# Other transfer estimates in an issue planner, and y loads on strands of their own

## The chip, the cores and the metric

One program runs on one core of one Trainium2 chip. The metric is the time of one execution in microseconds (us) on the device. Engines are named as the profile names them: PE (matmul), PEld (the weight loads that go with it), DVE (vector), ACT (scalar), POOL (GpSimd) and SP, whose queue issues all DMAs of this kernel.

## The reference

Two layers of a backbone. Each layer normalises 256 context rows and 1024 latent rows of width 1024, projects them into the inputs of four mixers, joins the four results to y, and projects y back:

```python
for l in range(DEPTH):                       # 2 layers
    need_ctx = l < DEPTH - 1
    ...                                      # mod, sh, sc, gt from c and c_ctx
    hx = _rms(x, norm_w[l]) * (1.0 + sc[:, None, :]) + sh[:, None, :]
    hc = _rms(ctx, norm_w[l]) * (1.0 + sc_c) + sh_c
    ux = _split(hx @ w_in[l], [M_COLS, A_COLS, G_COLS, D_COLS])
    uc = _split(hc @ w_in[l], [M_COLS, A_COLS, G_COLS, D_COLS])
    outs = [_mlstm_mixer(...), _diff_mixer(...), _gla_mixer(...), _gdn_mixer(...)]
    yx = jnp.concatenate([o[1] for o in outs], axis=-1)
    x = x + gt[:, None, :] * (yx @ w_out[l])
    if need_ctx:
        yc = jnp.concatenate([o[0] for o in outs], axis=-1)
        ctx = ctx + gt_c * (yc @ w_out[l])
return x
```

The mixers are an mLSTM, a differential attention, a gated linear attention (GLA) and a gated delta net (GDN); each gives 256 of the 1024 columns of y.

## The kernel before

The 1280 rows are ten tiles of 128 (layer 1 needs the eight latent tiles alone). Everything between stages (the projections, the mixers' inputs, y as `yd`, half-finished sums as `xp`) goes through DRAM.

The order of the instructions is not written by hand. While the program is built, each piece of the work is a strand (a thread) with a rank, and the class `Issue` records every operation through its `__call__` (the line L406 on which nearly all instructions of the profile stand). For each it works out, with numbers of its own, how long the operation takes on its engine (`dur`) and when its result can be read (`fin`); `choose` lets the strand go on whose next operation could start first, ranks breaking near ties. What comes out is one fixed list of instructions per engine, and for SP one fixed list of DMAs. These numbers are used only to order; the chip's own waits are semaphores. A strand asks for another's result with `need` and announces its own with `set`. `evac`, `sub` and `mulv` also use the planner's clock to choose between two engines, so the engine of a copy or a product can change with the numbers.

For a DMA the planner takes 0.475 us to issue (`dur`), then a start 0.65 us later or when the transfer ahead of it is through, bytes / 360e3 us of transfer and 1.0 us to land. For an ACT activation it takes a fixed part and an element count; loading the table of another function costs nothing in it.

The output projection has two halves. `out_first` multiplies the columns of attention and GDN (blocks 2, 3, 6, 7 of y) with `w_out`, adds the residual and stores `xp`; it runs beside GLA and the mLSTM. `outproj` does blocks 0, 1, 4, 5 (mLSTM and GLA), adds `xp`, and, in layer 0, normalises the sum for the next layer. Each half loads a tile of y (`out_load`, 128 rows by 512 columns, 256 KB, tile `y`, two buffers), turns it with four transposes on PE (`tr<-k_ident,y`), splits it into `yT` on ACT and DVE (`out_turn`), and multiplies (24 matmuls `o<-w,yT` or `o<-wo,yT`). In both, one strand `turns` does load and turn:

```python
for i in range(n):
    if "m" in parts:
        q_.need((l, "mlstm", i))
    if i > 1:
        q_.need((l, "o", i - 2, 1))
    todo[i] = out_load(L, L.yt[i], ks, op)
    ...
    out_turn(todo[i], ks, op, pps)
```

So the load of tile i stands behind the last matmul of tile i-2, and its turn right behind the load. The mLSTM, which runs at the same time, loads for each tile `pd` (512 KB), `kq` (512 KB), `mv`, `wb` and `oz`, and stores its part of y (`y<-hy`); its matmuls are `pp`, `m`. Other names in the rows: `KT` are the keys of the attention (`sc` its scores), `wm` the modulation weights (`mod`), `raw`, `rtmp`, `gsp` and `al` tiles of the gates' and GDN's front on which ACT runs Ln and Exp, `st` the residual tile of `out_first`, `x` that of `outproj`.

Of the kernel before, what the change touches and what calls it, by code (L numbers as in the profile page):

```python
# [16 lines left out]
AF = mybir.ActivationFunctionType  # L17
# [123 lines left out]
class Issue:  # L141
# [8 lines left out]

    def __init__(self):
        self.cols, self.psum = {}, set()
        self.shape, self.port = None, {"V": collections.deque(maxlen=12), "G": collections.deque(maxlen=12)}
        self.window, self.cool = collections.deque(), False
        self.now = dict.fromkeys("PVSGD", 0.0)
        self.link = 0.0
        self.past, self.slot, self.free = {}, {}, {}
        self.depth, self.gone = {}, {}
        self.done = set()
        self.strands, self.me, self.fault = [], None, None  # L160
        self.main = threading.Semaphore(0)
        self.log = None
# [46 lines left out]
    def note(self, name, box, wrote, end):  # L209
        a, b, c, d = box  # L210
        old = self.past.setdefault(name, [])
        old[:] = [u for u in old if not (u[4] == wrote and u[5] <= end and a <= u[0] and u[1] <= b and c <= u[2] and u[3] <= d)]
        old.append((*box, wrote, end))


    def run(self, *strands):
# [86 lines left out]
                self.give()  # L303
                self.me.wait = None

    def set(self, name):
        self.done.add(name)


    def __call__(self, e, op, fn, a, k):  # L310
# [49 lines left out]
                dur += n * 0.006  # L360
        elif e == "S":
            dur = (0.05 if op == "copy" else 0.09) + n / 1200 + (0.09 if "accum_out" in k or "bias" in k else 0)
        elif e == "G":
            r = 2.2 if op == "tensor_tensor" else 0.85 if op == "memset" else 0.93
            if ALU.pow in a:
                r = 165
            dur = 0.12 + n * r / 1000
        else:
            dur = 0.475
# [19 lines left out]
        end = start + dur  # L389
        if port:  # L390
            self.port[e].append((start, end))
        if e == "D":
            self.link = max(self.link, end + 0.65) + math.prod(outs[0][2].shape) * 4 / 360e3
            fin = self.link + 1.0
        else:
            fin = end + self.LAG[e]
        self.now[e] = end
# [32 lines left out]
def _build(tc, nc, A, out, root, dbg):  # L430
# [2225 lines left out]
    def out_first(L, wp, end):  # L2656
# [27 lines left out]
        def ev(*k):  # L2684
            return (l, "of", *k)

        def turns():
            mark(f"{l}out.first")
            for i in n:
                if i > 1:  # L2690
                    q_.need(ev("p", i - 2, 1))
                bs[i] = out_load(L, L.yt[i], ks, O.p)
                out_turn(bs[i], ks, O.p, O.ps)
                bs[i].ps = {}
                q_.set(ev("yT", i))

        def evacs():
            mark(f"{l}out.first")
# [7 lines left out]
            for i in n:  # L2706
# [10 lines left out]
                    q_.set(ev("e", i, nh))  # L2717
                dma(xp[l][128 * t:128 * t + 128, :], xs[i])
                q_.set((l, "first", t))
        q_.spawn(RANK["first turn"], turns)  # L2720
        q_.spawn(RANK["first turn"], evacs)
        for i in n:
# [11 lines left out]
    def outproj(L):  # L2734
# [5 lines left out]
        with ExitStack() as st:  # L2740
# [17 lines left out]
            def turns():  # L2758
                mark(f"{l}out.turn")
                for i in range(n):  # L2760
                    if "m" in parts:
                        q_.need((l, "mlstm", i))
                    if i > 1:
                        q_.need((l, "o", i - 2, 1))
                    todo[i] = out_load(L, L.yt[i], ks, op)
                    todo[i].i, todo[i].ps = i, {}
                    out_turn(todo[i], ks, op, pps)
                    q_.set((l, "yT", i))
                q_.set((l, "turns"))

            def place(t):
                g = next(g for g, (t0, n_) in enumerate(GRP) if t0 <= t < t0 + n_)
# [82 lines left out]
            def finishes():  # L2855
# [10 lines left out]
                for i, t in enumerate(L.yt):  # L2866
# [13 lines left out]
                    else:  # L2880
                        dma(x1[t], b.x)
                    q_.set((l, "fins", i))
            q_.spawn(RANK["out turn"], turns)
            q_.spawn(RANK["out turn"], finishes)
            if end:
# [55 lines left out]
```

## Time and profile before

| | |
|---|---|
| median of 3 runs | 2452.58 us (2437.7 to 2453.14) |
| profiled execution | 2444.86 us, its span 2443.0 us |
| PE busy | 2141.1 us (88% of the span) |
| DVE, ACT, POOL busy | 1513.1, 987.4, 850.4 us |
| DMA | 335.37 MB, 137 GB/s in the mean |
| chain that ended last | PE 55%, DMA 13%, DVE 11%, issue 8%, ACT 6%, SP queue 5% |
| mean granted clock of TensorE | 0.937 |

The span runs from the first instruction to the last. Busy shares are means over stages with different limits: layer 0 ends at about 1365 us, and in each layer the stage with the mLSTM and the output projection comes last.

### The profile page before, as it was taken

What the parts mean: (1) busy time and instruction counts of PE and PEld (TensorE: products, weight loads), DVE (VectorE), ACT (ScalarE), POOL (GpSimd) and SP (SyncE); (2) the same over time, 40 slices, a digit from 0 to 9 for tenths busy, and PEclk for the clock granted to TensorE, in tenths of its full rate; (3) what the DMA queues carried; (4) which work ended last, traced back from release to release, by engine and by line L of the source; (5) the groups of instructions that cost most, each with busy time, mean ns of one, the idle gap of its engine ahead of it and who ended that gap; (6) DMA issues with size and microseconds to landing.
All of it is one profiled execution on the core that took longest, in us unless ns stands there. A gap on an engine that the chain in (4) does not pass through costs nothing.

```text
span 2443.0 us, 57689 instructions
## 1 busy us (share of the span) xinstructions
PE 2141.1 (88%) x23367; PEld 1762.3 (72%) x23367; DVE 1513.1 (62%) x2676; ACT 987.4 (40%) x2169; POOL 850.4 (35%) x1075
## 2 busy tenths in 40 slices
PE   5899999999898998886868798889999989977888
PEld 1656778888776687865756677888888667866776
DVE  3586679555386854546556396686642778555665
ACT  2346412333376853222424255412322677533240
POOL 1343523554122225241522163623442122254340
PEclk8899999999999999988989899999999999976989
DMA  7347643455513134157953135432444331353694
GB/s 260 116 133 228 198 140 109 138 152 157 143 46 91 51 84 147 51 143 213 279 178 133 43 124 173 158 113 93 148 149 126 91 100 38 75 152 85 186 277 172
DMA packets 348051, 335.37 MB, mean 137 GB/s; under 512 B 93146, under 2 KB 292282, under 8 KB 347274
## 3 DMA queue, kind: packets, MB, share of 16 engines
q1 hardware_dynamic: 347786, 331.69, 45.6%
q8 instruction: 185, 3.03, 0.5%
q14 instruction: 80, 0.66, 0.1%
HBM read 226.78 MB, written 107.43 MB: 137 GB/s over the span
## 4 chain that ended last, share of the span: by engine, by line
PE 55%; DMA 13%; DVE 11%; issue 8%; ACT 6%; SPq 5%; POOL 2%; ACTq 0%; POOLq 0%; DVEq 0%
PE mm L406 26%; PE po L406 5%; SPq L406 5%; PE tr L406 4%; PE o L406 4%; PE sc L406 3%; PE p L406 3%; PE pd L406 3%; DVE st L406 2%; DMA wm<-in_w_mod 2%; PE puw L406 2%; ACT p L406 2%; PE m L406 2%; DVE cacc L406 1%; DMA KT<-akh 1%
## 5 line engine op out<-in xcount | busy, mean ns | idle before, releaser
L406 PE MATMUL mm<-w,hT 128*128 128x256 f32 x4512 | 645.6, 294 | 20.7 <-DVE st L406 10.0
L406 PEld LDWEIGHTS mm<-w,hT 128*128 128x128 f32 x4512 | 580.9, 195 | 52.9 <-issue 20.4
L406 PE MATMUL mm<-hT,w 128*128 128x512 f32 (+1 forms) x1680 | 388.9, 377 | 19.0 <-DVE w L406 4.9
L406 PEld LDWEIGHTS mm<-hT,w 128*128 128x128 f32 x1680 | 283.1, 195 | 90.0 <-issue 19.6
L406 DVE TENSOR_REDUCE st<-sc 128x1 f32<-128x1024 f32 (+1 forms) x200 | 200.2, 1027 | 69.8 <-PE sc L406 68.3
L406 ACT ACTIVATE p<-sc,st 128x256 f32<-128x256 f32 (+1 forms) x272 | 211.3, 786 | 68.8 <-DVE st L406 54.8
L406 POOL TENSOR_TENSOR w<-wr,w 128x512 fp32r<-128x512 f32 x62 | 87.4, 1411 | 235.5 <-ACT w L406 199.4
L406 POOL TENSOR_TENSOR hss<-hss,mhalf 128x2 f32<-128x2 f32 (+2 forms) x72 | 105.7, 1467 | 181.7 <-DVE hss L406 175.8
L406 PE MATMUL o<-wo,yT 128*128 128x512 f32 x540 | 155.2, 425 | 8.6 <-DVE x L406 7.1
L406 PE MATMUL sc<-KT,qt 96*128 96x512 f32 (+1 forms) x400 | 124.9, 402 | 30.3 <-DMA KT<-akh 13.3
L406 POOL TENSOR_TENSOR ss<-ss,mhalf 128x1 f32<-128x1 f32 (+1 forms) x39 | 68.2, 1749 | 193.4 <-DVE ss L406 185.4
L406 PEld LDWEIGHTS o<-wo,yT 128*128 128x128 f32 x540 | 105.7, 202 | 34.7 <-issue 5.6
L406 ACT COPY st<-mm 128x512 f32<-128x512 f32 (+1 forms) x83 | 45.8, 552 | 202.0 <-PE mm L406 140.9
L406 ACT COPY wt<-tr 128x512 f32<-128x512 f32 (+1 forms) x200 | 102.2, 511 | 60.4 <-PE tr L406 59.8
L406 PE MATMUL o<-w,yT 128*128 128x512 f32 x324 | 107.3, 462 | 21.8 <-DVE st L406 12.3
L406 PE MATMUL tr<-k_ident,p 128*128 128x128 f32 x656 | 114.7, 280 | 7.5 <-ACT wt L406 7.2
L406 POOL TENSOR_TENSOR st<-st 128x1 f32<-128x1 f32 (+1 forms) x136 | 26.6, 195 | 266.5 <-ACT p L406 196.9
L406 ACT CAST w<-wr 128x512 fp32r<-128x512 f32 x128 | 76.8, 620 | 103.7 <-PE mm L406 52.6
L406 PEld LDWEIGHTS sc<-KT,qt 96*128 96x128 f32 x400 | 63.8, 197 | 60.4 <-ACT p L406 32.0
L406 PE MATMUL po<-wt,av 128*64 128x128 f32 x1312 | 103.0, 282 | 2.0 <-DVE aacc L406 2.0
L406 DVE SCALAR_TENSOR_TENSOR p<-p,st,p 128x1280 f32<-128x1280 f32 (+1 forms) x72 | 103.0, 1431 | 2.6 <-POOL st L406 2.5
L406 DVE TENSOR_TENSOR w<-wr,w 128x512 fp32r<-128x512 f32 x66 | 59.1, 895 | 68.6 <-ACT w L406 64.9
(315 smaller groups left out, 4125.8 us busy)
## 6 DMA issues: line engine op xcount, KB each, us to landing
wr<-in_w_in SPq DMA_DIRECT2D x64, 512.0 KB
wm<-in_w_mod SPq DMA_DIRECT2D x64, 256.0 KB
y<-y SPq DMA_DIRECT2D x36, 256.0 KB
xp<-st SPq DMA_DIRECT2D x18, 512.0 KB
pd<-rs_NG SPq DMA_DIRECT2D x18, 512.0 KB
kq<-kq SPq DMA_DIRECT2D x18, 512.0 KB
x<-xp SPq DMA_DIRECT2D x18, 512.0 KB
wm<-in_w_mod SPq DMA_DIRECT2D x16, 512.0 KB
```

The source lines that it names most:

```text
L406: r = fn(*a, **k)
```

## The change

Three things change in the planner's numbers. A DMA's size is charged at 180 GB/s, or at 4.6 ns for each contiguous run of its smaller side (`run_of`) if that is more; 0.55 of this is what it holds the link for; and it lands 1.4 us after its issue plus the whole of it. An activation of another table than the last (Ln, or Exp and Tanh) is charged 1.28 us. And in both halves of the output projection the load of y moves from `turns` to a strand `fetches` of the same rank, which waits for the turn of tile i-2 and no longer for its products; `turns` keeps the wait for the products.

```diff
+    def run_of(x):
+        n = 1
+        for s, m in list(x.ap)[::-1]:
+            if m > 1:
+                if s != n:
+                    break
+                n *= m
+        return n
...
         elif e == "S":
             dur = (0.05 if op == "copy" else 0.09) + n / 1200 + (0.09 if "accum_out" in k or "bias" in k else 0)
+            table = {AF.Ln: "ln", AF.Exp: "exp", AF.Tanh: "exp"}.get(a[2] if len(a) > 2 else None)
+            if table and table != self.table:
+                dur += 1.28
...
         if e == "D":
-            self.link = max(self.link, end + 0.65) + math.prod(outs[0][2].shape) * 4 / 360e3
-            fin = self.link + 1.0
+            size = math.prod(outs[0][2].shape) * 4
+            run = min(self.run_of(a[0] if a else k["out"]), self.run_of(k["in_"] if "in_" in k else a[1])) * 4
+            own = max(size / 180e3, 0.0046 * size / run)
+            self.link = max(self.link, end + 0.65) + 0.55 * own
+            fin = max(self.link + 0.9, end + 1.4 + own)
...
             def turns():
                 mark(f"{l}out.turn")
                 for i in range(n):
+                    q_.need((l, "y there", i))
+                    if i > 1:
+                        q_.need((l, "o", i - 2, 1))
+                    out_turn(todo[i], ks, op, pps)
+                    q_.set((l, "y turned", i), (l, "yT", i))
+                q_.set((l, "turns"))
+
+            def fetches():
+                mark(f"{l}out.turn")
+                for i in range(n):
                     if "m" in parts:
                         q_.need((l, "mlstm", i))
                     if i > 1:
-                        q_.need((l, "o", i - 2, 1))
+                        q_.need((l, "y turned", i - 2))
                     todo[i] = out_load(L, L.yt[i], ks, op)
                     todo[i].i, todo[i].ps = i, {}
-                    out_turn(todo[i], ks, op, pps)
-                    q_.set((l, "yT", i))
-                q_.set((l, "turns"))
+                    q_.set((l, "y there", i))
...
+            q_.spawn(RANK["out turn"], fetches)
             q_.spawn(RANK["out turn"], turns)
```

`out_first` is changed in the same way. PE has the same 16175 matmuls and transposes after as before. Since the planner's numbers enter every choice, the whole program comes out in another order. Line L406 is L426 in the changed kernel, and the numbers in tile names differ between the two.

The first place is PE in layer 0, where `out_first` (`o<-w`, `o<-wo` of `yT_2340`) has ended and `outproj` begins (`y_14740` before, `y_14417` after, are its first tiles of y). Before:

```order
L406 MATMUL o_14680<-wo_2127_12933,yT_2340_14379 128x512
L406 MATMUL m_14697<-mv_2118_12920,pd_14574 128x65 x4
L406 MATMUL m_14713<-cs_2117_12919,wb_14580 128x130 x2
L406 MATMUL m_14713<-mv_2118_12920,pd_14574 128x65 x4
L406 MATMUL o_14680<-wo_2125_12931,yT_2341_14380 128x512
L406 MATMUL tr_14745<-k_ident_62,y_14740 128x128 x4
L406 MATMUL o_14787<-wo_2202_13621,yT_2397_14743 128x512
```

After:

```order
L426 MATMUL o_14350<-wo_2121_12785,yT_2304_14164 128x512
L426 MATMUL pp_14375<-kq_14262 128x128 x4
L426 MATMUL m_14390<-cs_2112_12769,wb_14265 128x130 x2
L426 MATMUL m_14390<-mv_2115_12772,pd_14259 128x65 x4
L426 MATMUL m_14403<-cs_2113_12770,wb_14265 128x130 x2
L426 MATMUL m_14403<-mv_2115_12772,pd_14259 128x65 x4
L426 MATMUL pp_14463<-kq_14377 128x128 x4
L426 MATMUL m_14471<-cs_2112_12769,wb_14380 128x130 x2
L426 MATMUL m_14471<-mv_2116_12773,pd_14374 128x65 x3
L426 MATMUL tr_14423<-k_ident_62,y_14417 128x128 x4
L426 MATMUL m_14471<-mv_2116_12773,pd_14374 128x65
```

Before, the first turn of `outproj` follows directly on the last product of `out_first`, with the mLSTM all but done; now two of the mLSTM's tiles (`pp`, `m`) stand between, and more of them behind.

The second place is SP at the same point: the stores of the mLSTM's y (`y<-hy`), its loads, the stores `xp<-st` of `out_first`, and the loads of y (`y<-y`). Before:

```order
L406 DMA y_31_108<-hy_14657 128x256
L406 DMA oz_14670<-oz_45_122 128x512
L406 DMA y_31_108<-hy_14711 128x256
L406 DMA xp_47_124<-st_14425 128x1024
L406 DMA y_14740<-y_31_108 128x2x256
L406 DMA y_31_108<-hy_14753 128x256
L406 DMA wr_14774<-in_w_in 128x4x256
L406 DMA wr_14779<-in_w_in 128x4x256
L406 DMA kq_44_121<-in_k_zero 64x2x1280
L406 DMA y_14785<-y_31_108 128x2x256
```

After:

```order
L426 DMA wb_14380<-rs_WI_197 64x4x128 x2
L426 DMA y_31_108<-hy_14365 128x256
L426 DMA oz_14395<-oz_45_122 128x512
L426 DMA xp_47_124<-st_14218 128x1024
L426 DMA y_14417<-y_31_108 128x2x256
L426 DMA y_14420<-y_31_108 128x2x256
L426 DMA y_31_108<-hy_14453 128x256
L426 DMA oz_14458<-oz_45_122 128x512
L426 DMA pd_14462<-rs_NG_196 128x8x128
L426 DMA kq_14473<-kq_43_120 128x8x128
```

The first two tiles of y are now loaded one behind the other, and loads of the mLSTM (`pd`, `kq`) stand behind them. In the whole program 27 of the 36 loads of y have loads of `pd` and `kq` of the same layer behind them on SP now (15 in layer 0, 12 in layer 1).

The third place is ACT in the front of layer 0, where `raw` (GDN) and `rtmp` (gates) get their Ln and Exp. Before:

```order
L406 ACTIVATE rtmp_1158<-rtmp_1158 128x1280
L406 ACT_TABLE_LOAD
L406 ACTIVATE rtmp_1158<-rtmp_1158 128x1280
L406 ACTIVATE raw_1043<-sq_1187,fixed_71 128x256
L406 ACTIVATE raw_1043<-sq_1202,fixed_71 128x512
L406 ACTIVATE raw_1043<-sq_1210,fixed_71 128x512
L406 ACT_TABLE_LOAD
L406 ACTIVATE raw_1043<-raw_1043 128x256
```

After:

```order
L426 ACTIVATE raw_981<-sq_1161,fixed_71 128x256
L426 ACT_TABLE_LOAD
L426 ACTIVATE raw_996<-cacc_1136 128x1284
L426 ACTIVATE rtmp_1213<-rtmp_794 128x1280
L426 ACT_TABLE_LOAD
L426 ACTIVATE raw_981<-sq_1182,fixed_71 128x512
L426 ACT_TABLE_LOAD
L426 ACTIVATE rtmp_1213<-rtmp_1213 128x1280
L426 ACT_TABLE_LOAD
L426 ACTIVATE raw_981<-sq_1239,fixed_71 128x512
```

The three activations on `sq` stood together and now change places with those on `rtmp`, with a table load at each change. Over the program ACT has 33 table loads after and 25 before.

## Rows read from the trace of the kernel before

**Rows 1.** The page: span, engines' busy time; a costly group: busy, mean ns | idle before it.

```profile
span 2443.0 us, 57689 instructions
PE 2141.1 (88%) x23367; PEld 1762.3 (72%) x23367; DVE 1513.1 (62%) x2676; ACT 987.4 (40%) x2169; POOL 850.4 (35%) x1075
...
L406 PE MATMUL o<-wo,yT 128*128 128x512 f32 x540 | 155.2, 425 | 8.6 <-DVE x L406 7.1
```

**Rows 2.** Windows of the last stages: length, engines' busy time, granted clock, DMA share, GB/s.

```profile
1050.00:1242.00 192.00, 148.05 (x1159) 121.15 (x1160) 106.64 (x208) 53.90 (x158) 65.89 (x91) 0.85 0.77 207
1242.00:1365.00 123.00, 88.77 (x405) 67.21 (x404) 67.13 (x118) 47.48 (x85) 24.08 (x20) 0.89 0.42 146
...
2300.00:2396.00 96.00, 82.52 (x419) 71.18 (x418) 64.05 (x126) 33.29 (x102) 38.76 (x49) 0.86 0.92 260
```

**Rows 3.** Waits of PE: us in total, times, longest us.

```profile
PE tr L406 <- DMA y<-y: 28.1, 11, 5.2
PE mod L406 <- DMA wm<-in_w_mod: 26.2, 22, 6.4
...
PE sc L406 <- DMA KT<-akh: 13.3, 3, 6.0
PE m L406 <- DMA kq<-kq: 12.8, 4, 7.2
PE o L406 <- DVE st L406: 12.3, 3, 7.0
...
PE pp L406 <- DMA kq<-kq: 4.1, 2, 2.2
...
PE sq L406 <- ACT raw L406: 1.7, 3, 1.0
```

**Rows 4.** Timeline of PE: start, length, instruction, [idle before it, releaser].

```profile
1053.93 1.12 PE L406 MATMUL tr<-k_ident,y 128*128 128x128 f32 x4 [4.01 <-DMA y<-y]
...
1134.04 2.50 PE L406 MATMUL o<-w,yT 128*128 128x512 f32 x5 [7.01 <-DVE st L406]
...
1239.09 1.11 PE L406 MATMUL tr<-k_ident,y 128*128 128x128 f32 x4 [5.20 <-DMA y<-y]
...
1255.78 0.93 PE L406 MATMUL tr<-k_ident,y 128*128 128x128 f32 x4 [4.95 <-DMA y<-y]
...
2328.53 1.12 PE L406 MATMUL tr<-k_ident,y 128*128 128x128 f32 x4 [4.18 <-DMA y<-y]
```

**Rows 5.** The chain that ended last: transfers from issue to landing (start, length).

```profile
640.59 11.06 DMA KT<-akh
...
1092.54 3.15 DMA y<-y
...
1104.79 5.23 DMA kq<-kq
...
1146.62 8.89 DMA kq<-kq
...
2400.95 7.12 DMA y<-y
```

**Rows 6.** Waits of SP's queue: us in total, times, longest us.

```profile
SPq L406 <- PE tr L406: 37.3, 14, 12.8
```

**Rows 7.** Timeline of ACT: a table load and the activation behind it.

```profile
139.44 1.28 ACT L406 ACT_TABLE_LOAD   x1
140.73 1.27 ACT L406 ACTIVATE rtmp<-rtmp 128x1280 f32<-128x1280 f32 x1
```

**Rows 8.** Windows of the same two stages in both layers (columns as in rows 2).

```profile
682.00:868.00 186.00, 171.60 (x1299) 132.03 (x1298) 149.97 (x278) 137.38 (x353) 51.31 (x117) 0.96 0.25 69
1922.00:2108.00 186.00, 171.58 (x1338) 132.76 (x1338) 154.71 (x271) 142.82 (x357) 48.84 (x115) 0.98 0.23 64
496.00:620.00 124.00, 117.63 (x1476) 103.92 (x1473) 66.86 (x160) 41.72 (x107) 62.31 (x71) 0.97 0.52 156
1736.00:1860.00 124.00, 122.27 (x1486) 102.28 (x1486) 61.14 (x159) 40.82 (x107) 54.03 (x67) 1.00 0.51 154
```

More of the change, by code (lines that the diff above doesn't have):

```diff
@@ L152, in __init__ @@
         self.cols, self.psum = {}, set()
+        self.table = None
         self.shape, self.port = None, {"V": collections.deque(maxlen=12), "G": collections.deque(maxlen=12)}
@@ L213, in note @@
         old.append((*box, wrote, end))
+    @staticmethod
+    def run_of(x):
[6 more added lines that the diff above has]
+        return n
     def run(self, *strands):
@@ L304, in need, with set @@
                 self.me.wait = None
-    def set(self, name):
-        self.done.add(name)
+    def set(self, *names):
+        self.done.update(names)
     def __call__(self, e, op, fn, a, k):
@@ L391, in __call__ @@
             self.port[e].append((start, end))
+        if e == "S" and op != "copy" and table:
+            self.table = table
         if e == "D":
-            self.link = max(self.link, end + 0.65) + math.prod(outs[0][2].shape) * 4 / 360e3
-            fin = self.link + 1.0
+            size = math.prod(outs[0][2].shape) * 4
[3 more added lines that the diff above has]
+            fin = max(self.link + 0.9, end + 1.4 + own)
         else:
@@ L2689, in turns @@
             for i in n:
+                q_.need(ev("y", i))
                 if i > 1:
                     q_.need(ev("p", i - 2, 1))
+                out_turn(bs[i], ks, O.p, O.ps)
+                q_.set(ev("turned", i), ev("yT", i))
+        def fetches():
+            mark(f"{l}out.first")
+            for i in n:
+                if i > 1:
+                    q_.need(ev("turned", i - 2))
                 bs[i] = out_load(L, L.yt[i], ks, O.p)
-                out_turn(bs[i], ks, O.p, O.ps)
                 bs[i].ps = {}
-                q_.set(ev("yT", i))
+                q_.set(ev("y", i))
         def evacs():
@@ L2719, in evacs @@
                 q_.set((l, "first", t))
+        q_.spawn(RANK["first turn"], fetches)
         q_.spawn(RANK["first turn"], turns)
@@ L2760, in turns, with fetches @@
                 for i in range(n):
+                    q_.need((l, "y there", i))
+                    if i > 1:
+                        q_.need((l, "o", i - 2, 1))
+                    out_turn(todo[i], ks, op, pps)
+                    q_.set((l, "y turned", i), (l, "yT", i))
+                q_.set((l, "turns"))
+            def fetches():
+                mark(f"{l}out.turn")
+                for i in range(n):
                     if "m" in parts:
```

## The prediction

> **What bounds the kernel now.** The page comes first: the span is 2443.0 us and PE is busy for 2141.1 us of it, no other engine for more than 1513.1 [rows 1]. So PE sets the pace and the question is what its 301.9 idle us wait for. The sum is made against the profiled execution, 2444.86 us, 7.7 us under the median of the runs shown (2452.58) and inside their range; that range is 0.6% wide, so 1% is about what a measurement of this kernel can tell from no change.
>
> The windows then show where the idle time lies: in the two stages with the mLSTM and the output projection PE is idle for 44.0 of 192 us, 34.2 of 123 and 13.5 of 96, at a granted clock of 0.85 to 0.89 of full speed, while the DMA engines are up to 92% busy [rows 2]. The list of PE's waits names what ended it. The largest item is a turn of `y` that waits for its load: 28.1 us in 11 waits. Other transfers follow: `wm` 26.2, `KT` 13.3, and `kq` 12.8 and 4.1 [rows 3]. The timeline shows the long ones: the turn stands first in PE's list, and nothing else is done until the tile is there [rows 4]. The chain gives what a transfer really takes from issue to landing, 3.15 to 7.12 us for a tile of y and 5.23 to 8.89 for `kq` [rows 5].
>
> **The change part by part.** First, the loads of y. Before, a load waits for the last matmul of tile i-2 and its turn follows at once; now it waits for the turn of tile i-2 and so goes out a whole product earlier. A tile's product is 24 matmuls at a mean of 425 ns [rows 1], 10.2 us, and the mean of the two loads in the rows is 5.1 us [rows 5], so a load issued that early is normally over. Of the 28.1 us, the first (4.01 us at 1053.93) belongs to the first tile of `out_first`, which has no tile before it to hide behind; it stays. The three longest others (5.20, 4.95, 4.18; together 14.3) go: two loads stand one behind the other now, and at 1239 us, where nothing covered the load, the new order has two tiles of the mLSTM's matmuls in front of the turn [rows 4]. Of the remaining 9.8 I count half, 4.9, since what is late next there is the evacuation of the last product (`o` behind `DVE st` 12.3 us, behind `DVE x` 7.1 [rows 1, 3]). That gives -19 us; the bounds are 0 and -28.1. The cover is the product of tile i-1 and the mLSTM; if it is gone, the load costs its 3 to 7 us again.
>
> Second, the estimates. By the diff, the planner's landing for `kq` of 512 KB in runs of 512 bytes goes from 3.58 to 6.58 us (these are its own numbers; they only order). The two rows have 5.23 and 8.89, 7.06 in the mean [rows 5], so it was 3.48 us short and is 0.48 short now: 86% of the misjudgment goes. Of the 16.9 us of PE's waits for `kq` that is 14.6 if other work is always ready to be put in front; I take half, -7 (bounds 0 and -14.6). For `KT` of 640 KB it goes from 3.95 to 5.52, where the row has 11.06 [rows 5]: 1.57 of 7.11 us short, 22% of 13.3, so -3 (bounds 0 and -13.3). For the `wm` loads of 256 KB it goes from 2.85 to 3.33 only, so their 26.2 us stay (0, and -26.2 as the far bound).
>
> Third, ACT. The planner is told of the table's price and yet the order holds eight loads more, since the price goes into an operation's length and not into its turn. One load is 1.28 us and the next activation starts 1.29 us after it did [rows 7], so ACT gets 8 x 1.29 = 10.3 us more work. It is busy for 40% of the span [rows 1], and where the loads stand PE waits for ACT's `raw` for 1.7 us in all [rows 3]. So nearly all is covered by ACT's idle time and PE's projection; I take +2 (bounds 0 and 10.3; a gain is excluded, since a load does no work). The Trainium skill, ScalarE: Activation LUTs, section What ACT_TABLE_LOAD costs, counts a drain of about 1380 ns on top of the load, some 2.66 us for each switch; by that, eight would be an estimated 21.3 us of ACT's time. The trace does not show the drain: 1.28 us of load and the next activation 0.01 us behind it.
>
> Fourth, everything else is put in another order, which no row prices. The nearest rows are stages that both layers run: the attention had PE busy 171.60 and 171.58 us of 186, the scan of GDN 117.63 and 122.27 of 124 [rows 8]. So order alone moved a stretch by 0.0 and 4.6 us, 2.3 in the mean. The span is about 16 such stretches: with independent signs 4 x 2.3 = 9 us, all of one sign 37. I take 0, and +-37 as bounds. SP gets two DMAs more, one normalised tile that now goes through DRAM; they are within these bounds.
>
> The sum is -19 - 7 - 3 + 2 = -27: 2444.86 - 27 = 2418 us, 1.4% under the median.
>
> **The rivals.** *The waits only change their name.* In the stage of the output projection the DMA engines are 77 to 92% busy [rows 2] and products also wait for `st`, 7.01 us at one point [rows 4]. A tile of y that lands earlier pushes the `xp`, `st` and `kq` transfers back by as much, and PE stands before `o` instead of before `tr`. For it speaks that 207 to 260 GB/s flow there already, against it that the second stretch, with 34.2 idle us, has the DMA at 42%. Then only the +2 stays: 2447 us, +-25 for the new order.
>
> *SP stands in front of the early loads; slower.* SP issues its list in order. A load of y now waits on SP for the turn of tile i-2 on PE, with the mLSTM's `pd` and `kq` behind it; 27 of 36 loads stand so. Where SP waited for turns it did for 37.3 us in 14 waits, 2.66 us each [rows 6]. Twenty-seven of these are 71.9 us; with half of it on the path of the mLSTM, whose transfers are in the chain [rows 5], and no gain from y, the time is 2444.86 + 36 = 2481 us. It turns slower by over 1% (2477) when these waits put more than 32 / 27 = 1.2 us each on the path. Against it: the planner places each load where it expects the turn to be over. The Trainium skill names the mechanism (DMA: Bandwidth & Descriptors, section Anatomy of one DMA): a semaphore wait of a DMA is held on the issuing sequencer, before dispatch. The trace agrees, with 37.3 us of such waits on SP.
>
> *The tables are on the path.* If the front of each layer is bound by ACT's chain of Ln and Exp, the 10.3 us count in full: 2418 - 2 + 10 = 2426 us. By the page's price of 2.66 us it would be an estimated 2437.
>
> *A denser PE also gets its clock.* The three stretches of rows 2 have 319.3 us of PE work at a mean granted clock of 0.86; the stretches of rows 8, where PE is idle for 8% of the time or less, have 0.96 to 1.00. At 0.96 the work would take 319.3 x (1 - 0.86 / 0.96) = 33 us less. With half of it, 2418 - 16 = 2402 us.
>
> That the change does not do what it says is ruled out by the order: the loads do stand earlier.
>
> **How the numbers follow.** The forecast has a chance of 0.40, the renamed waits 0.27, SP in front 0.15, the clock 0.14, the tables 0.04. The likeliest gives 2418 us. Faster by over 1% is under 2428: three quarters of the forecast, nearly all of the clock's case, half of the tables' and a fifth of the renamed waits', 0.50. Slower by over 1% is over 2477: 0.11 of the SP case and 0.05 of the renamed waits with a bad order, 0.16. The rest, 0.34, is within 1%. The range leaves out a part of the clock's case with a lucky order below 2390, and most of the SP case above 2474.
>
> **What would show it.** In the profile after: PE's wait of `tr` for `y` falls from 28.1 to under 9 us with the first tile's 4 us left; waits for `kq` fall to about 10 and `KT` to about 10; `o` waits for `DVE st` and `DVE x` stay below 25 together; PE's idle time falls by about 27; ACT shows 33 table loads and PE waits for `raw` for under 6 us. If `tr` waits little but `o` or `m` wait for what y waited for before, it was renamed; if SP's wait for `PE tr` grows past 70 us and `pd` and `kq` land later, the SP case holds. The forecast is wrong above all if another stage, one that this sum leaves at 0, comes out worse by more than the 27 us.

## The result and the profile after

The changed kernel takes 2462.91 us in the median (2454.64 to 2471.42), the kernel before 2446.26 us beside it: a ratio of 1.0074, 95% interval 1.0055 to 1.0092. The forecast was 2418 us, a gain of 1.4%; the time lies inside the range given, on the other side of the kernel before. The profiled execution took 2471.42 us, the longest of its runs, so its distance to the profile before (26.6 us) is more than the medians' 17.

The page after, answering to [rows 1]: span, busy time, chain.

```profile
span 2469.6 us, 57660 instructions
PE 2158.0 (87%) x23367; PEld 1774.0 (72%) x23367; DVE 1507.7 (61%) x2672; ACT 998.2 (40%) x2175; POOL 835.9 (34%) x1081
...
PE 59%; DVE 11%; DMA 9%; issue 8%; ACT 7%; SPq 3%; POOL 3%; POOLq 0%; ACTq 0%; DVEq 0%
```

PE is idle for 2469.6 - 2158.0 = 311.6 us, 9.7 more than before, and busy for 16.9 us more with the same 23367 instructions: the mean granted clock went from 0.937 to 0.928, and 2141.1 x 0.937 is 2158.0 x 0.928 within 0.2%. So this pair of profiles has two parts, idle time and clock; which of them belongs to the change, one pair cannot tell: the kernel before alone, in the 106 executions beside the runs below, had clocks of 0.927 to 0.941 and took 2431 to 2460 us. DMA's part of the chain fell from 13% to 9%. The loads of `y` and `kq`, 27.8 and 33.1 us of the chain before, are not in it after; those of `wm` rose from 46.1 to 62.5 us and those of `pd` from 13.5 to 23.8.

The waits of PE after, answering to [rows 3], say so (us in total, times, longest):

```profile
PE pd L426 <- issue: 30.2, 22, 2.4
PE mod L426 <- DMA wm<-in_w_mod: 25.2, 23, 3.4
PE tr L426 <- DVE x L426: 19.4, 10, 6.2
PE mm L426 <- DVE st L426: 19.3, 12, 4.9
PE o L426 <- DVE st L426: 16.4, 6, 6.5
...
PE m L426 <- POOL wb L426: 13.3, 5, 5.3
...
PE sc L426 <- DMA KT<-akh: 7.2, 2, 4.3
PE tr L426 <- DMA prow<-in_gla_b: 7.2, 1, 7.2
...
PE pd L426 <- DVE us L426: 5.9, 1, 5.9
...
PE m L426 <- DMA kq<-kq: 4.0, 1, 4.0
...
PE o L426 <- DVE x L426: 3.5, 2, 3.3
...
PE pp L426 <- DMA kq<-kq: 3.2, 1, 3.2
```

The wait for `y`, 28.1 us before, is no longer in the view; `kq` went from 16.9 to 7.2 us, `KT` from 13.3 to 7.2. In their place stand waits that were smaller or absent: `m` for `wb` (a 128 KB load that POOL multiplies), `o` for `DVE st` (12.3 before), `tr` for `DVE x`, `pd` for `DVE us`, and a turn of `prow` at the start of the program. Two of them before:

```profile
PE tr L406 <- DVE x L406: 16.3, 7, 5.9
...
PE m L406 <- POOL wb L406: 1.4, 2, 0.8
```

Where these new waits stand is seen in PE's timeline after, which answers to [rows 4]: start, length, instruction, [idle before it, releaser].

```profile
1067.50 1.12 PE L426 MATMUL tr<-k_ident,y 128*128 128x128 f32 x4
...
1147.65 4.18 PE L426 MATMUL o<-w,yT 128*128 128x512 f32 x9 [6.52 <-DVE st L426]
...
1215.00 1.28 PE L426 MATMUL m<-cs,wb 128*128 128x130 f32 x4 [5.35 <-POOL wb L426]
...
1237.77 1.17 PE L426 MATMUL m<-cs,wb 128*128 128x130 f32 x4 [3.86 <-POOL wb L426]
```

The turns of `y` have no idle time before them, not even the first; but in the same stage PE now waits for the evacuation of the product and for the mLSTM's `wb`. POOL's timeline shows what comes ahead of the product on `wb` there:

```profile
1211.98 1.01 POOL L426 TENSOR_TENSOR hss<-hss,mhalf 128x4 f32<-128x4 f32 x1 [4.46 <-DVE hss L426]
1213.53 0.73 POOL L426 TENSOR_TENSOR hy<-hy,oz 128x256 f32<-128x256 f32 x1 [0.54 <-DVE hy L426]
1214.22 1.41 POOL L426 TENSOR_TENSOR wb<-wb,kq 128x256 f32<-128x256 f32 x2
...
1236.02 1.01 POOL L426 TENSOR_TENSOR hss<-hss,mhalf 128x4 f32<-128x4 f32 x1 [3.19 <-DVE hss L426]
1237.00 1.59 POOL L426 TENSOR_TENSOR wb<-wb,kq 128x256 f32<-128x256 f32 x2
```

The product on `wb` has no idle time before it, so POOL is not seen to wait for that load; the product stands on POOL's list behind `hss`, which waited for DVE. As far as the trace shows, these waits come from POOL's order, which the planner also makes. The windows after, of layer 0's output stages and of the attention in both layers, answer to [rows 2, 8] (length, busy times, clock, DMA share, GB/s):

```profile
1057.44:1208.05 150.61, 126.20 (x1182) 99.90 (x1174) 83.48 (x148) 38.46 (x102) 44.43 (x63) 0.85 0.75 206
1208.05:1372.73 164.68, 126.09 (x609) 100.74 (x609) 88.82 (x180) 64.85 (x146) 53.31 (x53) 0.85 0.57 176
...
696.00:882.00 186.00, 171.61 (x1286) 132.12 (x1284) 146.85 (x277) 134.53 (x347) 52.39 (x116) 0.96 0.25 68
1932.00:2118.00 186.00, 170.07 (x1240) 131.26 (x1240) 152.76 (x265) 132.47 (x330) 42.66 (x110) 0.95 0.24 63
```

In the output stages PE is still idle for 24.4 and 38.6 us, at a clock of 0.85. The attention is as before. What is new lies at the beginning. The windows of the front of layer 0, up to the first load of GDN's scan (`kvl<-dk`), and of the rest; first the kernel before:

```profile
0.00:451.72 451.72, 393.83 (x3436) 293.96 (x3436) 293.91 (x451) 168.27 (x272) 159.34 (x146) 0.95 0.51 164
451.72:2443.00 1991.28, 1747.30 (x19931) 1468.35 (x19931) 1219.17 (x2226) 819.12 (x1897) 691.07 (x929) 0.93 0.45 131
```

and the changed kernel:

```profile
0.00:473.66 473.66, 401.66 (x3489) 302.62 (x3490) 287.41 (x451) 175.35 (x275) 152.34 (x150) 0.94 0.49 157
473.66:2469.60 1995.94, 1756.36 (x19879) 1471.38 (x19879) 1220.26 (x2221) 822.83 (x1900) 683.55 (x931) 0.93 0.45 132
```

The front is 21.9 us longer, with 72.0 us of idle time against 57.9 (and 53 matmuls more in it): +14.1, more than the whole program's +9.7. Everything behind it has 4.4 us less idle time than before.

The lateness of the front has a place in the trace. The function `gates` loads three strips of `w_in` (`graw`, 64, 128 and 64 KB, in contiguous runs of 64 or 128 bytes), each followed by the DVE copies `zz<-graw`; then ACT makes `wg` of `zz`, and PE multiplies by it. Timelines of SP, DVE, ACT and PE before:

```profile
92.06 0.43 SPq L406 DMA_DIRECT2D graw<-in_w_in  x1
96.23 0.39 SPq L406 DMA_DIRECT2D graw<-in_w_in  x1
97.47 0.45 SPq L406 DMA_DIRECT2D graw<-in_w_in  x1
...
95.01 0.30 DVE L406 COPY zz<-graw 128x64 f32<-128x64 f32 x2 [3.81 <-DMA graw<-in_w_in]
100.43 0.29 DVE L406 COPY zz<-graw 128x256 f32<-128x256 f32 x1 [5.11 <-DMA graw<-in_w_in]
101.42 0.30 DVE L406 COPY zz<-graw 128x64 f32<-128x64 f32 x2 [0.70 <-DMA graw<-in_w_in]
...
107.67 3.03 PE L406 MATMUL mm<-hT,wg 128*128 128x256 f32 x24
```

and after:

```profile
93.22 0.43 SPq L426 DMA_DIRECT2D graw<-in_w_in  x1
101.51 0.40 SPq L426 DMA_DIRECT2D graw<-in_w_in  x1
108.70 0.45 SPq L426 DMA_DIRECT2D graw<-in_w_in  x1
...
104.71 0.29 DVE L426 COPY zz<-graw 128x256 f32<-128x256 f32 x1 [3.92 <-DMA graw<-in_w_in]
...
114.70 1.05 ACT L426 CAST wg<-zz 128x1024 fp32r<-128x1024 f32 x1
...
122.68 2.99 PE L426 MATMUL mm<-hT,wg 128*128 128x256 f32 x24
```

From issue to the copy that waited for it a strip takes 2.95, 4.20 and 3.95 us before, and 3.20 in the one row after in which DVE waits for it. The planner's old formula said 2.31 and 2.49, the new one says 6.58: 1024 runs x 4.6 ns + 1.4 + 0.475. Since load and copies are one strand, the planner now expects each copy 6.6 us behind its load and puts the next load behind that: the three are issued within 15.5 us instead of 5.4, and the gates' first matmul comes 15.0 us later.

### The profile page after: what moved, and what is told of

Same layout as the page of the kernel before. It is cut to its first block, busy times and chain, and to the rows that moved or that the text cites. A ratio compares the mean times of both kernels' runs of the same rounds, so it can differ in the third digit from the quotient of the medians.

```text
span 2469.6 us, 57660 instructions
## 1 busy us (share of the span) xinstructions
PE 2158.0 (87%) x23367; PEld 1774.0 (72%) x23367; DVE 1507.7 (61%) x2672; ACT 998.2 (40%) x2175; POOL 835.9 (34%) x1081
## 4 chain that ended last, share of the span: by engine, by line
PE 59%; DVE 11%; DMA 9%; issue 8%; ACT 7%; SPq 3%; POOL 3%; POOLq 0%; ACTq 0%; DVEq 0%
PE mm L426 25%; PE o L426 6%; PE po L426 6%; PE tr L426 4%; PE sc L426 4%; PE pd L426 4%; SPq L426 3%; PE p L426 3%; DMA wm<-in_w_mod 3%; PE m L426 2%; ACT p L426 2%; PE puw L426 2%; PE mod L426 1%; DVE st L426 1%; DMA KT<-akh 1%
## 5 line engine op out<-in xcount | busy, mean ns | idle before, releaser
L426 PE MATMUL mm<-w,hT 128*128 128x256 f32 x4512 | 647.3, 294 | 29.6 <-DVE st L426 11.9
L426 PEld LDWEIGHTS mm<-w,hT 128*128 128x128 f32 x4512 | 583.3, 195 | 62.4 <-issue 21.3
L426 PE MATMUL mm<-hT,w 128*128 128x512 f32 (+1 forms) x1680 | 396.8, 382 | 21.0 <-DVE st L426 7.3
L426 PEld LDWEIGHTS mm<-hT,w 128*128 128x128 f32 x1680 | 285.2, 198 | 94.1 <-issue 23.7
L426 DVE TENSOR_REDUCE st<-sc 128x1 f32<-128x1024 f32 (+1 forms) x200 | 200.0, 1026 | 83.6 <-PE sc L426 82.1
L426 ACT ACTIVATE p<-sc,st 128x256 f32<-128x256 f32 (+1 forms) x272 | 212.0, 789 | 66.9 <-DVE st L426 47.1
L426 POOL TENSOR_TENSOR hss<-hss,mhalf 128x2 f32<-128x2 f32 (+2 forms) x72 | 100.3, 1394 | 231.1 <-DVE hss L426 230.8
L426 POOL TENSOR_TENSOR w<-wr,w 128x512 fp32r<-128x512 f32 x61 | 88.4, 1449 | 215.9 <-ACT w L426 154.0
L426 PE MATMUL o<-wo,yT 128*128 128x512 f32 x540 | 155.0, 427 | 3.7 <-DVE x L426 3.5
L426 PE MATMUL sc<-KT,qt 96*128 96x512 f32 (+1 forms) x400 | 126.6, 405 | 30.5 <-ACT p L426 12.4
L426 ACT COPY wt<-tr 128x512 f32<-128x512 f32 (+1 forms) x200 | 102.7, 513 | 74.8 <-PE tr L426 74.1
L426 POOL TENSOR_TENSOR ss<-ss,mhalf 128x1 f32<-128x1 f32 (+1 forms) x39 | 68.3, 1751 | 182.3 <-DVE ss L426 182.0
L426 ACT COPY st<-mm 128x512 f32<-128x512 f32 (+1 forms) x75 | 41.6, 554 | 218.1 <-PE mm L426 178.1
L426 PEld LDWEIGHTS o<-wo,yT 128*128 128x128 f32 x540 | 106.7, 204 | 29.1 <-DVE x L426 4.5
L426 PE MATMUL tr<-k_ident,p 128*128 128x128 f32 x656 | 115.5, 281 | 9.5 <-ACT wt L426 9.3
L426 PE MATMUL o<-w,yT 128*128 128x512 f32 x324 | 105.6, 468 | 19.6 <-DVE st L426 16.4
L426 POOL TENSOR_TENSOR st<-st 128x1 f32<-128x1 f32 (+1 forms) x136 | 26.8, 197 | 274.7 <-ACT p L426 193.3
L426 ACT CAST w<-wr 128x512 fp32r<-128x512 f32 x128 | 77.8, 622 | 100.2 <-PE mm L426 63.5
L426 PE MATMUL po<-wt,av 128*64 128x128 f32 x1312 | 107.2, 285 | 2.5 <-DVE aacc L426 2.5
L426 PEld LDWEIGHTS sc<-KT,qt 96*128 96x128 f32 x400 | 65.0, 200 | 57.3 <-ACT p L426 30.3
L426 DVE SCALAR_TENSOR_TENSOR p<-p,st,p 128x1280 f32<-128x1280 f32 (+1 forms) x72 | 104.0, 1444 | 2.9 <-POOL st L426 2.9
L426 PEld LDWEIGHTS tr<-k_ident,p 128*128 128x128 f32 x656 | 75.7, 141 | 36.2 <-ACT wt L426 20.9
```

Source lines behind the costliest of these rows:

```text
L426: r = fn(*a, **k)
```

## Experiments

The theories named in the expectations: **A**, the new DMA numbers cost time in the fronts and the strands gain; **B**, the table price costs it; **C**, the early loads of y cost it on SP; **D**, it is the price of the `graw` loads that delays the front; **E**, any small change of a number deals the later stages anew, and the total is a draw; **F**, the front is late for modulation weights and tables. Ratios are to the kernel before, with their 95% intervals; "idle" is the span less PE's busy time in the profile.

**One part at a time.** The changed kernel with the other parts taken back (here for the strands alone; the other two correspondingly, and one with only the table price taken back).

```diff
-            if table and table != self.table:
-                dur += 1.28
...
-            size = math.prod(outs[0][2].shape) * 4
-            run = min(...) * 4
-            own = max(size / 180e3, 0.0046 * size / run)
-            self.link = max(self.link, end + 0.65) + 0.55 * own
-            fin = max(self.link + 0.9, end + 1.4 + own)
+            self.link = max(self.link, end + 0.65) + math.prod(outs[0][2].shape) * 4 / 360e3
+            fin = self.link + 1.0
```

> The kernel before with the strands for y alone, its old DMA numbers and no table price. Up to the output projection of layer 0 its order is that of before. Theory A (the new DMA numbers cost the time, in the front of each layer; the strands gain in the output projection): ratio to before 0.990 to 0.996, K loads of layer 0 at their old 219 us. Theory B (the table price costs it): the same, 0.990 to 0.996. Theory C (the early loads of y cost it, on the queue of SP): 1.005 or more.

> The kernel before with the new DMA numbers alone, y loaded and turned in one strand, no table price. Theory A: ratio 1.010 to 1.018, the loads of K in layer 0 some 30 us later than in before (219 us). Theory B: 0.995 to 1.003, K at 215 to 225 us. Theory C: 0.990 to 1.000.

> The kernel before with the price of 1.28 us for a table of another function alone. Theory A: ratio 0.997 to 1.003. Theory B: 1.010 to 1.018, with the loads of K in layer 0 some 30 us later. Theory C: 0.997 to 1.003.

> The changed kernel without the table price: strands and DMA numbers stay. Theory A: ratio to before 1.005 to 1.012, as the changed kernel (1.0074), K of layer 0 still late, at 245 us or more. Theory B: 0.990 to 0.998, K back at 215 to 225 us. Theory C: as the changed kernel, 1.005 to 1.010.

Measured: the strands alone 0.9995 (0.9970 to 1.0019), the DMA numbers alone 1.0001 (0.9982 to 1.0019), the table price alone 0.9990 (0.9962 to 1.0018), strands and DMA numbers together 1.0150 (1.0105 to 1.0194). No part loses by itself, and two of them lose twice what all three do. Of the ratios that A and B gave for the four, each misses three, and C's fit no better. So these four name no culprit; they fit E. The traces say more than the times: with the DMA numbers the front is late in each (the first `bcol` load, which stands behind the gates' copies, +16.4 us with the numbers alone, +16.5 with the strands), without them it is not (+0.3 with the table price alone, 0.0 with the strands alone). One profile does not fit in: with the table price alone the gates are in time, but the first load of `K` stands 18.5 us later than before, the front has 65.7 us of idle time and the whole 311.5, at a ratio of 0.9990. It was built at this one setting only, so what the table price does to the order stays open.

**The same kernels at other settings.** To tell a loss of the change from a draw, two numbers of the planner were moved by an amount that means nothing to the chip, in the kernel before and in the changed one:

```diff
-            dur = 0.475
+            dur = 0.477
```

or

```diff
-    LAG = {"P": 0.2, "V": 0.13, "S": 0.14, "G": 0.08}
+    LAG = {"P": 0.2, "V": 0.132, "S": 0.14, "G": 0.08}
```

> The kernel before with 0.477 us instead of 0.475 for the planner's issue of a DMA, a change of no meaning that draws another order. Theory E: ratio off 1 by 0.003 to 0.012, either way. Theory D (each effect has its own cause and the order as such does little): 0.998 to 1.002.

> The kernel before with 0.132 us instead of 0.130 for the planner's lag behind a DVE instruction, again of no meaning. Theory E: ratio off 1 by 0.003 to 0.012, either way. Theory D: 0.998 to 1.002.

> The changed kernel with 0.477 us instead of 0.475 for the planner's issue of a DMA. Theory E: anywhere from 0.995 to 1.015 of before. Theory D: 1.005 to 1.010, as the changed kernel, with the gates' first matmuls at 120 to 126 us.

> The changed kernel with the lag of 0.132. The change is at 1.0074 with the old numbers and at 1.0107 with the issue of 0.477. If the change has a loss of its own (theories A and D: the front begins 16 us late for the gates' loads), it is above the 1.0057 that the same lag gives without the change, by 0.7 to 1%: 1.012 to 1.016. Theory E alone: a draw, as likely below 1.0057 as above it.

Measured: the kernel before 1.0010 (0.9992 to 1.0028) and 1.0057 (1.0036 to 1.0078), the changed one 1.0107 (1.0076 to 1.0137) and 1.0090 (1.0064 to 1.0116). So 2 ns in one number alone move the time by up to 0.6%, as E says, though 1.0010 lies in D's band. The changed kernel is behind the kernel before at each of three settings, by 0.74, 0.97 and 0.33%, 0.68% in the mean. The last is less than half of the 0.7 to 1% that A and D expected there, and three draws that scatter like this make a loss of the change's own likely, not sure. The strands and the DMA numbers alone went through the same settings.

> The kernel before with the strands of the y loads alone, and the planner's cost of a DMA issue set to 0.477 instead of 0.475. With that number alone the kernel before came to 1.001, with the strands alone to 0.9995. Theory S (the strands have an effect of their own, which the later stages pass on): 0.0005 below 1.001, between 0.999 and 1.002. Theory E (any small change of a number deals the order of the later stages anew, and the total moves by some 0.5% either way): outside that band as likely as inside it, anywhere in 0.995 to 1.011.

> The strands alone, with the planner's lag behind a VectorE instruction set to 0.132 instead of 0.13. With that number alone the kernel before came to 1.0057. Theory S: 1.005, between 1.003 and 1.007. Theory E: a draw of its own, 0.995 to 1.011, so more likely below 1.003 than in the band.

> The new DMA numbers alone, with the issue cost of 0.477. Without the new numbers this setting gives 1.001, with the whole change 1.0107. Theory A2 (the new numbers lose by themselves, and the 1.0001 measured for them alone was a lucky order): 1.006 to 1.012, TensorE idle above 312 us. Theory I (the loss is in the strands and the numbers together, neither alone): 0.998 to 1.004.

> The new DMA numbers alone, with the lag of 0.132. Without them this setting gives 1.0057, with the whole change 1.009. Theory A2: 1.008 to 1.015, TensorE idle above 312 us. Theory I: 1.003 to 1.008, idle below 310 us.

Measured: the strands 0.9969 (0.9943 to 0.9995) and 1.0027 (1.0009 to 1.0045), the DMA numbers 1.0174 (1.0126 to 1.0222) and 1.0065 (1.0040 to 1.0090). The strands come out ahead of the kernel before at all three settings, by 0.05, 0.41 and 0.30%, but the first is within the noise and both of the others lie outside the bands of theory S (0.9969 and 1.0027, both below): a gain is likely, its size is open. The DMA numbers alone are behind it by 0.01, 1.64 and 0.08%: A2's band of 1.006 to 1.012 was overshot at the first new setting, with 335.9 us idle (above 312, as A2 said), and at the second the ratio of 1.0065 lies in the band of theory I, the 314.6 us of idle time in that of A2. Only one of the three losses is clear of the noise, and three values as far apart as these do not give the DMA numbers' loss a size.

**The price of the three strips.** The changed kernel with only these loads charged by their size:

```diff
             own = max(size / 180e3, 0.0046 * size / run)
+            if outs[0][0].startswith("graw"):
+                own = size / 180e3
```

> The changed kernel, with the six loads of the gates' weights (graw) charged by size alone, so that their runs of 64 and 128 bytes cost nothing extra in the planner; the arithmetic is the same. Theory D (the price for short runs puts these three loads one after the other far apart, and with them the gates, on which the front of layer 0 waits): the gates' first matmuls at 105 to 112 us instead of 122.7, the loads of K at 228 to 240 instead of 250.7, ratio to before 0.995 to 1.003. Theory E (the total is decided by the luck of the order in the later stages; the front is one draw among several): the front comes back as in D, but the ratio may be anywhere from 0.99 to 1.015. Theory F (the front is late for the modulation weights, or for the tables): gates at 118 or later, ratio 1.004 to 1.011.

> The changed kernel with the gates' loads charged by their size alone, at the issue cost of 0.477, where the changed kernel itself is at 1.0107. Theory D (the price of these loads costs about 0.3%, as 1.0074 against 1.0042 without the new setting): 1.007 to 1.008, TensorE idle about 10 us below the 327 of the changed kernel there. Theory E (the 0.3% was a draw): anywhere from 1.003 to 1.014, with no preference for less than 1.0107.

> As the run before, at the lag of 0.132, where the changed kernel itself is at 1.009. Theory D: 1.005 to 1.007, TensorE idle about 10 us below 324. Theory E: 1.002 to 1.013, with no preference for less than 1.009.

Measured: 1.0042 (1.0018 to 1.0066), 0.9972 (0.9951 to 0.9993) and 0.9917 (0.9889 to 0.9945), below the changed kernel by 0.32, 1.35 and 1.73%. The gates' first matmul is back at 109.4, 110.1 and 108.6 us and the first load of `K` at 232.6 us in the first of them, as D (and E) said; F falls. D's ratios (0.995 to 1.003, 1.007 to 1.008, 1.005 to 1.007) were missed all three times, the first by too small a gain, the others by too large a one, and PE's idle time fell by 29 to 30 us there instead of 10: the sign is right each time, the size is not D's. At the lag of 0.132 this is the fastest kernel of the study and faster than both kernels; how much of that is its order, one setting does not say.

**The loads first.** All the new numbers kept, but the three strips are requested before the first copy, so the planner cannot put one load behind another's copy:

```diff
+                raws = []
                 for (col, n, src) in (...):
-                    raw = wp([128, 8, 32], "graw", 3)
-                    dma(raw[:, :, :n], ...)
+                    raws.append((wp([128, 8, 32], "graw", 3), src))
+                    dma(raws[-1][0][:, :, :n], ...)
+                for raw, src in raws:
                     for (so, wd, do) in src:
```

> The changed kernel, with the three loads of the gates' weights written ahead of the copies that read them, so that the planner, whatever it charges for one, has all three under way at once. Theory D (the short-run price of these loads, three times in a row, makes the front late): the gates' first matmul comes back from 122.7 us to about 108, the first load of K from 250.7 to 235 or less, and the total comes to 1.002 to 1.006, as with the price left at the size alone (1.0042). Theory E: the front comes back too, but the total is a draw, 0.997 to 1.013. If the front does not come back, it is not these loads' price but the other new numbers, and D falls.

> The changed kernel with the gates' three loads written ahead of their copies, all the new numbers kept, at the issue cost of 0.477, where the changed kernel is at 1.0107 and with these loads charged by size at 0.9972. Theory D1 (it is the serial placing of the three loads that costs, however it is removed; the 1.0114 at the old setting was an unlucky order): below 1.004. Theory D2 (the high price costs in another way too, as a wrong picture of the link or of the second layer's gates): 1.005 to 1.014.

> As the run before, at the lag of 0.132, where the changed kernel is at 1.009 and with these loads charged by size at 0.9917. Theory D1: 0.990 to 1.002. Theory D2: 1.004 to 1.013.

Measured: 1.0114 (1.0091 to 1.0137), 1.0151 (1.0116 to 1.0186) and 1.0017 (0.9999 to 1.0036). PE's timeline in the first of them has the gates' matmuls at 109.65 us:

```profile
109.65 2.95 PE L426 MATMUL mm<-hT,wg 128*128 128x256 f32 x23
```

So the serial placing is gone, as meant, and the first load of `K` is back at 230.0 us there, as D said; but the ratio misses D's 1.002 to 1.006, and the total is no better than the changed kernel's at two of three settings: +0.40, +0.44, -0.73%. D1 falls at 0.477, where D2's band is overshot too; at the lag of 0.132 the time lies in D1's band. As a full account D1 is not borne out. The table, with what the traces add, shows what each of the two edits gives back. Idle time is that of three profiles, one of each order; the front is the part up to the first `kvl<-dk`, the last stage that from layer 1's first `gk<-gqk` load (GLA) to the end.

| kernel | ratio at the old setting, 0.477, 0.132 | mean | idle, us | mean | front | last stage |
|---|---|---|---|---|---|---|
| before | 1, 1.0010, 1.0057 | 1.0022 | 301.9, 306.8, 304.4 | 304.4 | 60.3 | 56.8 |
| strands alone | 0.9995, 0.9969, 1.0027 | 0.9997 | 292.2, 298.3, 301.0 | 297.2 | 60.8 | 52.5 |
| the change | 1.0074, 1.0107, 1.0090 | 1.0090 | 311.6, 326.9, 323.6 | 320.7 | 70.7 | 60.6 |
| DMA numbers alone | 1.0001, 1.0174, 1.0065 | 1.0080 | 309.4, 335.9, 314.6 | 320.0 | 68.4 | 60.8 |
| `graw` by size | 1.0042, 0.9972, 0.9917 | 0.9977 | 301.6, 297.4, 293.9 | 297.6 | 60.1 | 56.2 |
| loads first | 1.0114, 1.0151, 1.0017 | 1.0094 | 320.2, 319.6, 309.8 | 316.5 | 65.0 | 65.3 |

The means of idle time part the kernels as the means of the ratios do: three below 305 us with 0.998 to 1.002, three above 316 us with 1.008 to 1.009. What the three above have in common is the new price of the strips. Each single order bears it out: the nine with this price have 309.4 to 335.9 us of idle time (with strands and DMA numbers together, 326.4), the nine without it 292.2 to 306.8; only the table price alone, with 311.5, reaches that range without the strips' new price. The ratios overlap, 1.0001 to 1.0174 against 0.9917 to 1.0057, with means of 1.0088 and 0.9999. Busy time does not part them: its means of three lie between 2139.6 and 2146.1 us, while single profiles go from 2133.0 to 2158.0. So of the 16.9 us of busy time between the first two profiles 6.5 are left in the means; the 16.3 us of idle time between the change and the kernel before are the steadier part. Of these, 10.4 us lie in the front. Charging the strips by size takes all 10.4 away, and 12.5 us more behind the front; the loads written first take 5.7 of the front's and give 4.7 back in the last stage. How the price costs behind the front was not found; in layer 1 the three strips are issued within 1.2 us in every order.

The windows at the setting of 0.477 show this in single rows. The changed kernel has 68.3 us of idle time up to the scan:

```profile
0.00:466.99 466.99, 398.65 (x3489) 303.25 (x3490) 290.31 (x451) 175.07 (x275) 155.65 (x150) 0.94 0.50 159
466.99:2467.00 2000.01, 1741.47 (x19879) 1460.81 (x19879) 1221.33 (x2234) 829.50 (x1904) 681.81 (x920) 0.93 0.46 134
```

with the strips charged by size 56.5:

```profile
0.00:450.69 450.69, 394.19 (x3516) 300.69 (x3517) 284.11 (x446) 173.11 (x276) 153.88 (x142) 0.96 0.52 165
450.69:2438.00 1987.31, 1746.44 (x19852) 1464.78 (x19852) 1215.87 (x2217) 827.39 (x1914) 686.74 (x931) 0.93 0.47 136
```

and with the loads first 65.4, though this front is as short:

```profile
0.00:451.19 451.19, 385.75 (x3421) 291.15 (x3422) 289.52 (x444) 166.35 (x267) 159.79 (x146) 0.94 0.51 162
451.19:2467.90 2016.71, 1762.52 (x19947) 1480.27 (x19947) 1222.73 (x2211) 835.67 (x1924) 696.16 (x934) 0.93 0.46 134
```

It is as short because 95 matmuls fewer stand in it (3421 against 3516; 8.4 us less of busy time against 8.9 us more of idle time); they come later, and behind the front it is 29.4 us longer. A landmark that is reached early is no gain by itself; the idle time up to it is.

## Why the prediction was wrong

**The loads of y: the mechanism right, the gain mis-sized.** The step counted -19 us, with half of the remaining wait kept for "the evacuation of the last product". The waits of PE, as means over the three settings, show the wait for `y` falling from 27.7 us to 6.6 with the strands alone and to 0.2 with the change, as forecast (under 9). It falls to 5.2 with the DMA numbers alone too, so the first two terms of the sum were not independent. And the strands alone lower PE's idle time by 7.2 us, not by 19 or 21: `tr` behind `DVE x` grows by 7.6 us and `o` behind `DVE st` by 7.5. Two thirds of the gain changed their name. "What is late next" was asked for the remaining 9.8 us alone, and it should have been asked for the 14.3 us that were counted in full.

**The estimates: right in size, given back beside it.** `kq` was to fall by 7 and `KT` by 3; the means of three fall by 7.4 (13.5 to 6.1) and 3.6 (16.5 to 12.8). At the same time `m` behind `POOL wb` rises from 2.5 to 17.9 and `o` behind `DVE st` from 8.8 to 19.9, both in the output stages, and `pd` of GLA behind `DVE us` from 0.3 to 8.9. Together these 35.0 us nearly consume the 38.6 that `y`, `kq` and `KT` gave. That does not make them the loss: with the strips charged by size `wb` and `st` cost as much (16.6 and 20.8 us), and that kernel is not slower. The mark for `o` behind `st` and `x`, below 25 us together, held in the first profile (19.9) and not at the lag of 0.132 (27.6). This is the rival of the renamed waits, which had 0.27 and 2447 us; I gave it too little, although [rows 4] showed `o` behind `st` for 7.01 us in the very stage. Its forecast of nearly no gain was near: without the strips' price the whole change has 6.8 us less idle time than the kernel before, where the three terms of `y`, `kq` and `KT` had 29.

**ACT's tables: +2 neither borne out nor contradicted.** The table price alone measured 0.9990, with 9.6 us more idle time in its one profile. ACT's timeline after, answering to [rows 7], has the load and the next activation again right behind each other:

```profile
141.61 0.47 ACT L426 ACTIVATE raw<-sq,fixed 128x256 f32<-128x256 f32 x1 [7.34 <-PE sq L426]
142.11 1.28 ACT L426 ACT_TABLE_LOAD   x1
143.40 1.27 ACT L426 ACTIVATE raw<-cacc 128x1284 f32<-128x1284 f32 x1
```

PE's wait for ACT's `raw`, 1.7 us before, is not in the view after, so the mark "under 6 us" holds there (at the setting of 0.477 the wait is 6.5 us). The Trainium skill, ScalarE: Activation LUTs, section What ACT_TABLE_LOAD costs, would have a drain of about 1380 ns on top. These rows have no room for one: the load starts 0.03 us after the activation before it has ended, and the next activation 0.01 us after the load.

**Everything else in another order: the step that failed.** It was taken at 0 with bounds of 37 us. It measured 23.1 us of idle time as the price of the three strips alone, in both layers (320.7 us against 297.6 without it, means of three), of which 10.6 us lie in the front; with the -6.8 us that the rest of the change brought, this makes the +16.3 that stand against the -27 of the sum. The 0 came from two stages that both layers run [rows 8]. Both are stages in which PE is busy for 92 to 99% of the time. The front of layer 0 is not one of them: it had 57.9 us of idle time in 451.7 us before, with a chain of load, copy, cast and matmul that the planner's numbers lengthen. The change moved a number of that chain from 2.31 to 6.58 us, where the traces have 2.95 to 4.20; the diff and the trace before held both, and the prediction compared the new estimates with the trace for `kq` and `KT` only, loads that PE was seen to wait for. Under the old numbers the strips were priced too low, and PE was not seen to wait for them. Their new price, not their time, made the front late, and 10.4 of the 16.3 us of added idle time lie there. That the price costs is shown at three settings, its size only as a mean that scatters (0.32, 1.35 and 1.73%); that it costs by the serial placing alone is not, since the loads written first remove the placing and half of the front's idle time but not the loss. Where the last stage of those kernels gets its 65.3 us (the kernel before has 56.8) was not found. Nor is the price of the strips the only new wait in the front: in all 13 orders with the new DMA numbers, the strips charged by size among them, the turn of `prow` at 21 us waits for its load for 6.5 to 7.4 us, and in none of the others.

**The rivals.** SP's wait for turns grew as that case said, but it did not decide:

```profile
SPq L426 <- PE tr L426: 70.1, 19, 10.8
```

It was 37.3 us in 14 waits [rows 6], and 70 was the mark (51.0 and 78.4 us at the other settings). But `kq` was not later for it, since PE's wait for it fell. For `pd` POOL waits: 53.7 us after against 41.1 before, but 38.9 against 39.6 as means of three. And the strands alone, with 79.4 us of SP's waits for turns, are not slower. The clock's case went the other way, 0.928 after 0.937, where executions of the kernel before alone lie between 0.927 and 0.941.

**The chances.** 0.34 for "within 1%", where it ended. A forecast of -27 us had 0.40; the errors are the two first parts, counted at 29 where about 7 stay, and the fourth, counted at 0. The 1.4% were partly no gain of the change at all: 7.7 us of them are the distance of the one profiled execution from the median of three. That the time lies inside the range is no merit of the sum; the range was wide enough for a loss that the sum did not have.

## What to carry to other kernels

When a planner's cost is corrected, compare the new number with the trace for every load that it moves most, not for those that the hardware waits for now: here the price of three small loads a layer cost more idle time (23.1 us) than all the rest of the change gave back (6.8 us). When the order of a whole program changes, one pair of times says little; move a number that means nothing by a hair in both kernels, and compare the means of idle time and of time over such settings. Where a wait is taken away in a stage that waits for several things in turn, ask of all of it what is late next, not of the small waits alone.

## What the runs showed of the hardware

One and the same program, the kernel before, took 2431 to 2460 us in 106 executions on five chips, at mean granted clocks of TensorE of 0.927 to 0.941. PE's busy time in the profiles of all orders, 2133.0 us (clock 0.939) to 2158.0 (0.928) for the same 23367 instructions, spreads by the same 1.2%. So a difference in busy time between two profiles need not be one of the orders.

A strip of 64 KB in runs of 64 bytes took 2.95 and 3.95 us from issue to its copy, one of 128 KB in runs of 128 bytes 4.20 and 3.20: the same 1024 runs, twice the bytes, and hardly longer. In the other runs the copies that waited for such a strip began 2.3 to 4.6 us after its issue, so the planner's 6.58 us is too high for both. The Trainium skill, DMA: Bandwidth & Descriptors, section Rules for kernel authors, says that under 64 KB one pays mostly overhead. No strip here is under 64 KB; that twice the bytes took hardly longer fits with it.
